# A two-layer decoder trunk on one core: the second MLP product in 16 full steps round a ring, last steps in turn, first six products side by side

## The chip, the cores and the metric

The kernel runs on one core of one Trainium2 chip. The metric is the device time of one execution in microseconds, as the median over several runs. The engines are called PE (matrix products), DVE (vector), ACT (scalar, activations and copies), POOL (general) and SP, whose queue issues most transfers. PSUM banks hold what PE accumulates; SBUF holds everything else.

## The reference

Each of the two layers does, on 1024 tokens of 1024 channels in f32 (positions, pooling and rotary tables left out here):

```python
for i in range(DEPTH):
    hn = rmsnorm(h, norm1[i])
    z = hn @ w_in[i]
    ...
    pool_out = pool_mixer(u, pool_w[i], pool_scale[i])
    attn_out = dilated_mixer(q, k, v)
    h = h + jnp.concatenate([pool_out, attn_out], axis=-1) @ w_out[i]
    hn = rmsnorm(h, norm2[i])
    h = h + jnp.square(jax.nn.relu(hn @ w_up[i])) @ w_down[i]
    gate = jax.nn.sigmoid(rmsnorm(h, norm3[i]) @ w_gate[i])
    h = h + gate * (p[i] @ w_ple[i])
return rmsnorm(h, final_norm)
```

`dilated_mixer` joins three head groups by a softmax over their log-sums; the MLP has 4096 inner channels, so `w_up` is 1024 x 4096 and `w_down` 4096 x 1024. The two products with them are what the change is mostly about.

## The kernel before, in words

**Numbers.** Every f32 operand of a large product is split into a high and a low part (fp32r). ACT makes the high part by a copy, DVE the low part by a subtraction, and PE does three matmuls of 128x128 by 128x512 for each pair of tiles (high-high, high-low, low-high).

**Seven products for eight.** The two MLP products are done in blocks of 2 x 2 tiles with seven products, P1 to P7, in place of eight. Class `Seven` prepares the weights: `load` (L261) fetches a set's raw blocks (names u0r, u1r for the up product of layer 0, d0r for the down product) by SP, `sums` (L274 to L287) makes four sums of blocks on POOL (u0s, d0s), `make` (L289 to L301) makes each of the seven pieces (u0p, d0p): ACT copies (L299), DVE subtracts (L301). `products7` (L527 to L537) issues the matmuls (L535). The other side of the product are the pieces xP (of the normalised residual, four row tiles, for the up product) and wP (of the squared ReLU, for the down product).

**The banks.** P1, P6, P5 and P3 of a set accumulate one after another in a bank X (three buffers), P7 and P4 in a bank Z (two), P2 in a bank Y (two); the order is P1, P7, P6, P2, P5, P4, P3. A product's result must be taken out of its bank (`close`) before the next product of that bank may go on in it. At one product of four row tiles, twelve matmuls, X's next product follows one other product later.

**Up product** (`class Up`, L1129 to L1182): 16 sets of 256 inner channels ("channel pairs"), seven products each over the four row tiles xs. `close` copies on ACT or adds on DVE into y, then ReLU times the norm factor on DVE (L1156), square on ACT (L1159), four differences ys on DVE (L1174 to L1180), and SP writes the seven pieces to x_d in memory.

**Down product** (`class Down`, L1199 to L1219): 19 steps of `STEPS`, triples (t, a, b): output pair t (of 4) takes row tiles a to b of the 16. The first three steps have 3, 2 and 1 row tiles, then come 13 steps of 4, then three with 3, 2 and 1. `close` adds a bank into an SBUF accumulator acc on DVE (L1212). `x_back` (L1189 to L1196) brings one wP piece of one row tile back: SP transfer, ACT copy (L1194), DVE low part (L1196). After each product of a step, one piece of one new row tile is fetched. When an output pair has its last row tile, `rest` splits the result for the gate product and adds its squares to the third norm.

**Around them.** Ahead of the up product lies the output projection (bank names po, evacuated by L1025 and L1048 on DVE into res), which needs the attention outputs. These are weighed with jt, a 96x128 transpose of the joint weights (L907), written to memory and spread by DMA (wb). Behind the down product comes the gate product (gt) with ss_c, the norm's column sums.

**What sets the order.** A class `Clock` runs generators on a simulated time at build, and the kernel's instructions come out in the order of that time; the numbers in the generators (`yield 900.0`) and in the lead times of `Seven` are delays in ns that decide only this order. On the chip every engine runs its own instructions in that order and waits on semaphores for the others.

Of the kernel before, what the change touches and what calls it, by code (L numbers as in the profile page):

```python
# [37 lines left out]
T_M1, W_0, W_1 = 13000.0, 6000.0, 1800.0  # L38
# [3 lines left out]
STEPS = [(3, 0, 3), (2, 0, 2), (1, 0, 1)] + [(a % 4, a, min(a + 4, 16)) for a in range(16)]  # L42
# [72 lines left out]
def body(nc, tc, pools, A, out):  # L115
# [107 lines left out]
    class Seven:  # L223
# [26 lines left out]

        def lead(self, ns, step):

            for q in sorted(k for k in self.kicks if k < 0):
                for fn in self.kicks[q]:
                    ck.at(max(0.0, ns + q * step), fn)

        def at(self, q):
            for fn in self.kicks.get(q, ()):
                fn()

        def load(self, j):  # L261
            src, k0, n, c0 = self.sets[j]
            self.raw[j] = []
            for t in range(2):
                r = blk(f"{self.name}r{t}", F32, (128, n, 2, 128))
                nc.sync.dma_start(out=r.rearrange("p i k c -> p (i k) c"),
                                  in_=src[256 * k0:256 * (k0 + n), c0 + 128 * t:c0 + 128 * t + 128]
                                  .rearrange("(k p) c -> p k c", p=128))
                self.raw[j].append(r)

# [3 lines left out]
        def sums(self, j):  # L274
            a11, a12, a21, a22 = (self.block(j, t, k) for t in range(2) for k in range(2))
            n = self.sets[j][2]
            s = [blk(f"{self.name}s0", F32, (128, 2, n, 128))]
# [1216 lines left out]
```

## Time and profile before

| | |
|---|---|
| median of 3 runs | 2368.24 us (2368.02 to 2368.82) |
| profiled execution | 2371.95 us |
| its span | 2370.2 us, mean granted clock of PE 0.988 |
| PE busy | 2296.6 us (97%) |
| DVE busy | 1704.2 us (72%) |
| ACT, POOL busy | 1008.5 us (43%), 709.3 us (30%) |
| stages of layer 1 | up 422.6 to 741.4 us, down 741.4 to 1067.5 us |
| stages of layer 2 | up 1585.4 to 1906.0 us, down 1906.0 to 2232.2 us |

The profile is one execution. Durations are those of its instructions; a wait is the time in which an engine stood still before an instruction, put down to what released it last. The granted clock of PE is given as a share of full speed: 0.5 is 1.2 GHz, 1.0 is 2.4 GHz. PE matmuls overlap, so a row's own length (0.39 us) is more than the distance between two starts. The rows that the prediction rests on stand below in their own section.

### The profile page before, as it was taken

What the parts mean: (1) busy time and instruction counts of PE and PEld (TensorE: products, weight loads), DVE (VectorE), ACT (ScalarE), POOL (GpSimd) and SP (SyncE); (2) the same over time, 40 slices, a digit from 0 to 9 for tenths busy, and PEclk for the clock granted to TensorE, in tenths of its full rate; (3) what the DMA queues carried; (4) which work ended last, traced back from release to release, by engine and by line L of the source; (5) the groups of instructions that cost most, each with busy time, mean ns of one, the idle gap of its engine ahead of it and who ended that gap; (6) DMA issues with size and microseconds to landing.
All of it is one profiled execution on the core that took longest, in us unless ns stands there. A gap on an engine that the chain in (4) does not pass through costs nothing.

```text
span 2370.2 us, 30970 instructions
## 1 busy us (share of the span) xinstructions
PE 2296.6 (97%) x11088; PEld 1850.2 (78%) x11088; DVE 1704.2 (72%) x2888; ACT 1008.5 (43%) x2161; POOL 709.3 (30%) x562
## 2 busy tenths in 40 slices
PE   8999999899999999989999999999999989999898
PEld 6767778788887788878887767887888868888788
DVE  7555657687778888886565466686777798888845
ACT  5244533443335344444324345334433354443545
POOL 5111126323331433341221122253233233332422
PEclk9999999999999999999999999999999999999999
DMA  5011133254448555521120112233444485553214
GB/s 178 19 46 19 38 90 107 67 165 158 155 150 282 162 159 158 150 67 45 59 58 19 37 37 56 81 116 98 154 156 156 152 289 151 159 156 107 85 54 134
DMA packets 292401, 268.31 MB, mean 113 GB/s; under 512 B 12092, under 2 KB 223672, under 8 KB 292248
## 3 DMA queue, kind: packets, MB, share of 16 engines
q1 hardware_dynamic: 289656, 262.70, 36.3%
q0 software_dynamic: 2272, 3.61, 0.9%
q8 instruction: 87, 1.43, 0.2%
q14 instruction: 66, 0.54, 0.1%
q10 hardware_dynamic: 320, 0.03, 0.0%
HBM read 193.65 MB, written 72.58 MB: 112 GB/s over the span
## 4 chain that ended last, share of the span: by engine, by line
PE 46%; DVE 5%; ACT 1%; POOL 1%; issue 1%; DMA 1%; SPq 0%; DVEq 0%; ACTq 0%; POOLq 0%
PE X L535 13%; PE Z L535 7%; PE Y L535 3%; PE in L520 3%; PE in L518 3%; PE in L522 3%; PE gt L522 2%; PE gt L518 2%; PE gt L520 2%; PE s L752 1%; PE o L788 1%; PE e L774 1%; PE pl L518 1%; PE pl L520 1%; PE pl L522 1%
## 5 line engine op out<-in xcount | busy, mean ns | idle before, releaser
L535 PE MATMUL X<-wP,d1p 128*128 128x512 f32 x768 | 187.6, 394 | 14.5 <-DVE acc L1212 13.9
L535 PE MATMUL X<-wP,d0p 128*128 128x512 f32 x768 | 188.5, 395 | 13.1 <-DVE acc L1212 12.0
L535 PE MATMUL X<-xP,u0p 128*128 128x512 f32 x768 | 185.5, 394 | 3.9 <-ACT y L1133 3.9
L535 PE MATMUL X<-xP,u1p 128*128 128x512 f32 x768 | 185.1, 393 | 3.9 <-ACT y L1133 3.9
L1196 DVE TENSOR_TENSOR wP<-wP 128x512 fp32r<-128x512 f32 x224 | 184.0, 824 | 3.9 <-ACT wP L1194 3.9
L535 PEld LDWEIGHTS X<-wP,d1p 128*128 128x128 f32 x768 | 144.3, 190 | 49.9 <-ACT d1p L299 9.0
L535 PEld LDWEIGHTS X<-wP,d0p 128*128 128x128 f32 x768 | 144.5, 190 | 49.2 <-ACT d0p L299 9.6
L535 PEld LDWEIGHTS X<-xP,u0p 128*128 128x128 f32 x768 | 145.9, 190 | 35.2 <-ACT y L1133 4.7
L535 PEld LDWEIGHTS X<-xP,u1p 128*128 128x128 f32 x768 | 145.4, 190 | 35.1 <-ACT y L1133 4.8
L1159 ACT ACTIVATE y<-y 128x1024 f32<-128x1024 f32 x64 | 67.5, 1055 | 221.9 <-DVE y L1156 221.9
L1194 ACT ACTIVATE wP<-wP 128x512 fp32r<-128x512 f32 x224 | 137.9, 620 | 40.5 <-DMA wP<-x_d 40.2
L188 DVE SCALAR_TENSOR_TENSOR wl<-wr,gt,wh 128x128 fp32r<-128x128 f32 (+1 forms) x288 | 118.8, 444 | 38.7 <-ACT wh L194 38.4
L647 POOL TENSOR_TENSOR rot<-rot,s 128x512 f32<-128x512 f32 x48 | 61.5, 1285 | 277.3 <-DVE rot L645 216.2
L1212 DVE TENSOR_TENSOR acc<-acc,X 128x512 f32<-128x512 f32 x152 | 103.6, 682 | 34.1 <-PE X L535 30.5
L765 ACT ACTIVATE sm<-sm,nm 128x128 f32<-128x128 f32 (+1 forms) x192 | 84.5, 442 | 93.1 <-DVE nm L762 92.9
L194 ACT ACTIVATE wh<-wr,gt 128x128 fp32r<-128x128 f32 (+1 forms) x304 | 104.2, 396 | 0.7 <-DMA wr<-in_w_in_dram 0.7
L758 DVE CUSTOM_DVE_ANT_0 sm<-s,cst 128x128 f32<-128x128 f32 (+1 forms) x192 | 58.3, 347 | 52.0 <-PE s L752 52.0
L535 PE MATMUL Z<-xP,u1p 128*128 128x512 f32 x384 | 95.0, 396 | 0.3 <-DVE xP L1011 0.2
L535 PE MATMUL Z<-xP,u0p 128*128 128x512 f32 x384 | 93.8, 392 | 0.3 <-DVE xP L1011 0.2
L535 PE MATMUL Z<-wP,d0p 128*128 128x512 f32 x384 | 93.5, 390 | 0.0
L535 PE MATMUL Z<-wP,d1p 128*128 128x512 f32 x384 | 93.4, 389 | 0.0
L535 PEld LDWEIGHTS Z<-xP,u1p 128*128 128x128 f32 x384 | 73.2, 191 | 16.3 <-DVE xP L1011 0.5
(474 smaller groups left out, 5969.0 us busy)
## 6 DMA issues: line engine op xcount, KB each, us to landing
wP<-x_d SPq DMA_DIRECT2D x224, 256.0 KB, 2.8
x_d<-ys SPq DMA_DIRECT2D x64, 512.0 KB, 3.5
wr<-in_w_in_dram SPq DMA_DIRECT2D x40, 512.0 KB, 3.8
u0r<-in_w_up_dram SPq DMA_DIRECT2D x32, 512.0 KB, 5.4
x_d<-y SPq DMA_DIRECT2D x32, 512.0 KB, 2.8
u1r<-in_w_up_dram SPq DMA_DIRECT2D x32, 512.0 KB, 5.6
d0r<-in_w_down_dram SPq DMA_DIRECT2D x26, 512.0 KB, 5.7
d1r<-in_w_down_dram SPq DMA_DIRECT2D x26, 512.0 KB, 5.7
```

What stands on the lines that cost most here:

```text
L188: nc.vector.scalar_tensor_tensor(l[:, k], raw[:, k], gs[k], f(h[:, k]), op0=OP.mult, op1=OP.subtract)
L194: nc.scalar.activation(h[:, k], raw[:, k], AF.Copy, scale=gs[k])
L518: nc.tensor.matmul(p, wh, h[:, cols], start=first and i == 0, stop=False)
L520: nc.tensor.matmul(p, wh, l[:, cols], start=False, stop=False)
L522: nc.tensor.matmul(p, wl, h[:, cols], start=False, stop=last and i == n - 1)
L535: nc.tensor.matmul(p, w[:, a, i], x[:, b], start=first and i == 0 and a == b == 0, stop=i == n - 1 and a == 1, skip_group_check=not first)
L647: nc.gpsimd.tensor_tensor(a, a, tb["s"][:, hs(hf)], op=OP.mult)
L765: nc.scalar.activation(sm[:, i, hh], sm[:, i, hh], AF.Exp, bias=nm[:, j:j + 1], scale=0.125, accum_out=ml[g][:, n, 4 + h:5 + h])
L1159: nc.scalar.activation(y, y, AF.Square)
L1194: nc.scalar.activation(t[:, 0], f(t[:, 1]), AF.Copy)
L1196: nc.vector.tensor_tensor(t[:, 1], f(t[:, 1]), f(t[:, 0]), op=OP.subtract)
L1212: nc.vector.tensor_tensor(a, a, p, op=OP.add)
```

## The change

1. **STEPS.** 16 steps of four row tiles each, in a ring: steps 2n and 2n+1 take the row tiles 2n to 2n+3 (wrapping behind 16) for two of the four output pairs, alternately pairs 0, 1 and 2, 3. Weights that wrap are loaded by two transfers. Pieces of two new row tiles are fetched in odd steps (`t % 2`), the second 5000 ns behind the first in the build's time; the first four row tiles are fetched during the last 14 up products.
2. **In turn.** The last two down steps, and the last two channel pairs of the up product, are issued product by product in turn (P1 of the one, P1 of the other, P7, P7, ...). What follows each finished result (`rest`) is collected in `ends` and handed out three at a time per product of the last step. The differences ys of the last two channel pairs come 24000 ns later in the build's time.
3. **Side by side.** The first six up products (P1, P2, P7 of two channel pairs) are interleaved on each row tile (before: four), and the last four output-projection results take banks of the kinds mm, o, e, e in place of s, s, e, e (s holds Y, e holds Z, mm holds X).
4. **Times.** `Seven` starts its parts by build time and no longer by product number; several delays change (the joint weights, the spreading, the norms, x_back).

```diff
+ORDER = ("P1", "P7", "P6", "P2", "P5", "P4", "P3")
+
+STEPS = [(2 * (i // 2 % 2) + i % 2, i // 2 * 2, 4) for i in range(16)]
...
+        def __init__(self, sets, seq, name, lead=(12, 6, 4), side=0):
             self.sets, self.seq, self.name = sets, seq, name
             load, sums, make = lead
             self.raw, self.sum, self.piece = {}, {}, {}
             self.first = {}
+            self.begin, t = [], 0.0
             for q, (j, _) in enumerate(seq):
                 self.first.setdefault(j, q)
-            self.kicks = {}
+                self.begin.append(t)
+                t += 675.0 * sets[j][2]
+            self.kicks = []
             for j, q in self.first.items():
-                self.kick(q - load, lambda j=j: self.load(j))
-                self.kick(q - sums, lambda j=j: ck.go(self.sums(j)))
+                self.kick(q, load, lambda j=j: self.load(j))
+                self.kick(q, sums, lambda j=j: ck.go(self.sums(j)))
             for q, (j, P) in enumerate(seq):
-                self.kick(q - make, lambda j=j, P=P: ck.go(self.make(j, P), (name, j, P)))
-
-        def kick(self, q, fn):
-            self.kicks.setdefault(q, []).append(fn)
-
-        def lead(self, ns, step):
-
-            for q in sorted(k for k in self.kicks if k < 0):
-                for fn in self.kicks[q]:
-                    ck.at(max(0.0, ns + q * step), fn)
-
-        def at(self, q):
-            for fn in self.kicks.get(q, ()):
-                fn()
+                fn = lambda j=j, P=P: ck.go(self.make(j, P), (name, j, P))
+                if q < side:
+                    self.kicks.append((-9000.0 + 1200.0 * q, fn))
+                else:
+                    self.kick(q, make, fn)
+            self.kicks.sort(key=lambda x: x[0])
...
+            yield 7000.0
...
-        first = [(0, "P1"), (1, "P1"), (0, "P2"), (1, "P2"), (0, "P7"), (0, "P6"), (1, "P7"), (0, "P5"),
-                 (1, "P6"), (0, "P4"), (1, "P5"), (0, "P3"), (1, "P4"), (1, "P3")]
+        first = [(j, P) for P in ("P1", "P2", "P7", "P6", "P5", "P4", "P3") for j in range(2)]
         n7 = len(sevens[L][0])
-        seq = first + [(j, P) for j in range(2, n7) for P in ("P1", "P7", "P6", "P2", "P5", "P4", "P3")]
-        S7 = Seven(sevens[L][0], seq, f"u{L}")
+        seq = first + [(j, P) for j in range(2, n7 - 2) for P in ORDER]
+        seq += [(j, P) for P in ORDER for j in (n7 - 2, n7 - 1)]
+        S7 = Seven(sevens[L][0], seq, f"u{L}", side=6)
...
-        outs = [(bank(f"po{L}", ("s", "e")[k // 2]), wk(ws[k % 2], range(8)), hs(k // 2)) for k in range(4)]
+        outs = [(bank(f"po{L}", ("mm", "o", "e", "e")[k]), wk(ws[k % 2], range(8)), hs(k // 2)) for k in range(4)]
...
+                if self.j >= n7 - 2:
+                    yield 24000.0
...
+            nc.sync.dma_start(out=f(t[:, 1]), in_=x_d[i % 16][PLACE[P]])
+            yield 6000.0
...
+                    if self.j >= nst - 4 and P in ("P2", "P3", "P4", "P5"):
+                        ends.append((self, a, m, hf))
...
+        def end(n):
+
+            for i in range(min(n, len(ends))):
+                s, a, m, hf = ends.pop(0)
+                if m not in hg3:
+                    hg3[m] = pair(f"g3_{m}_{L}")
+                ck.go(s.rest(a, m, hf), (id(hg3[m][0]), hf), 800.0 + 1300.0 * i)
+
+        nst = len(STEPS)
+        seq2 = [(k, P) for k in range(nst - 2) for P in ORDER]
+        seq2 += [(k, P) for P in ORDER for k in (nst - 2, nst - 1)]
         D7 = Seven(sevens[L][1], seq2, f"d{L}", (9, 6, 3))
...
-        run(S7, seq, range(4), live, lambda j: xs)
-        for q in range(4, len(seq)):
+        run(S7, seq, range(6), live, lambda j: xs)
+        for q in range(6, len(seq)):
             run(S7, seq, [q], live, lambda j: xs)
             if q == len(seq) - 8:
-                D7.lead(7 * 12 * 225.0, 2700.0)
-                early = [(i, P) for P in ORDER for i in range(3)] + [(3, P) for P in ORDER]
-                for n, (i, P) in enumerate(early):
-                    ck.at(3200.0 + 1150.0 * n, lambda i=i, P=P: ck.go(x_back(i, P)))
-
-
-        live = {k: Down(k) for k in range(len(STEPS))}
-        for q in range(len(seq2)):
-            k, P = seq2[q]
-            s = live[k]
+                D7.lead(8 * 12 * 225.0)
+            n = q - len(seq) + 15
+            if n > 0 and n % 2 == 0:
+                for i in range(4):
+                    ck.at(1500.0 * i + 300.0 * n, lambda i=i, P=seq[q][1]: ck.go(x_back(i, P)))
+
+
+        live = {k: Down(k) for k in range(nst)}
+        for q, (k, P) in enumerate(seq2):
+            t, a, n = STEPS[k]
             if P == "P1":
-                for m in (2 * s.t, 2 * s.t + 1):
+                for m in (2 * t, 2 * t + 1):
                     if acc[m] is None:
                         acc[m] = blk(f"acc{m}_{L}")
                         nc.sync.dma_start(out=acc[m], in_=h_d[m])
-                if s.b == 16:
-                    if norm3 is None:
-                        norm3 = Norm(f"c{L}")
-                    for m in (2 * s.t, 2 * s.t + 1):
-                        hg3.append(pair(f"g3_{m}_{L}"))
-            run(D7, seq2, [q], live, lambda k: xw[STEPS[k][1]:STEPS[k][2]])
-            if k >= 3 and s.a + 4 < 16:
-                ck.go(x_back(s.a + 4, P))
+                if k >= nst - 2 and norm3 is None:
+                    norm3 = Norm(f"c{L}")
+            run(D7, seq2, [q], live, lambda k: xw[a:a + n])
+            if t % 2 and k < nst - 2:
+                ck.go(x_back(a + 4, P))
+                ck.at(5000.0, lambda i=a + 5, P=P: ck.go(x_back(i, P)))
+            if k == nst - 1:
+                end(3 if P != "P3" else 16)
```

Three places show what moves. Line numbers are those of each kernel: L301 of before is L332 of the changed one, L1048 is L1079, L1050 is L1081, L1015 is L1046, L1196 is L1230, L1212 is L1242, L535 is L566. X, Y and Z are the banks, acc_0_... the accumulators of layer 0, po_3696 and po_3697 the results of the last output projection for the first half of the tokens, po_3698 and po_3699 for the second.

DVE, end of layer 0's output projection and start of its up product, before:

```order
L301 TENSOR_TENSOR u0p<-u0r_3701,u0p 128x512
L301 TENSOR_TENSOR u0p<-u0r_3705,u0p 128x512
L1048 TENSOR_TENSOR res_0_3856<-po_3696,h_6H 128x512
L1048 TENSOR_TENSOR res_0_3857<-po_3697,h_7H 128x512
L1050 TENSOR_TENSOR res_0_3856<-res_0_3856,h_6L 128x512
L1050 TENSOR_TENSOR res_0_3857<-res_0_3857,h_7L 128x512
L1015 SCALAR_TENSOR_TENSOR xP_3861<-res_0_3856,gt,xP_3861 128x512
L1015 SCALAR_TENSOR_TENSOR xP_3864<-res_0_3857,gt,xP_3864 128x512
L301 TENSOR_TENSOR u0p<-u0s_3756,u0p 128x512
L301 TENSOR_TENSOR u0p<-u0s_3779,u0p 128x512
L301 TENSOR_TENSOR u0p<-u0s_3775,u0p 128x512
L301 TENSOR_TENSOR u0p<-u0s_3756,u0p 128x512
```

The same place in the changed kernel:

```order
L332 TENSOR_TENSOR u0p<-u0r_3705,u0p 128x512
L332 TENSOR_TENSOR u0p<-u0s_3756,u0p 128x512
L332 TENSOR_TENSOR u0p<-u0s_3775,u0p 128x512
L1079 TENSOR_TENSOR res_0_3862<-po_3696,h_6H 128x512
L1079 TENSOR_TENSOR res_0_3863<-po_3697,h_7H 128x512
L1081 TENSOR_TENSOR res_0_3862<-res_0_3862,h_6L 128x512
L1081 TENSOR_TENSOR res_0_3863<-res_0_3863,h_7L 128x512
L1046 SCALAR_TENSOR_TENSOR xP_3867<-res_0_3862,gt,xP_3867 128x512
L1046 SCALAR_TENSOR_TENSOR xP_3870<-res_0_3863,gt,xP_3870 128x512
L1079 TENSOR_TENSOR res_0_3862<-po_3698,h_6H 128x512
L1079 TENSOR_TENSOR res_0_3863<-po_3699,h_7H 128x512
```

Two low parts of sums moved ahead of the first results, and the second half's results follow the first half's xP at once, where four low parts stood before. PE meanwhile, in the changed kernel, on the first row tile:

```order
L566 MATMUL X_3888<-xP_3271,u0p 128x512 x3
L566 MATMUL X_3889<-xP_3271,u0p 128x512 x3
L566 MATMUL Y_3890<-xP_3339,u0p 128x512 x3
L566 MATMUL Y_3891<-xP_3339,u0p 128x512 x3
L566 MATMUL Z_3892<-xP_3392,u0p 128x512 x3
L566 MATMUL Z_3893<-xP_3392,u0p 128x512 x3
```

Z comes as the 13th matmul; its two banks are those of po_3698 and po_3699. They were so before too, but there Z began behind all 48 matmuls of X and Y.

DVE inside the down product of layer 0, before, in a step of four row tiles:

```order
L1212 TENSOR_TENSOR acc_0_6512<-acc_0_6512,Y_7412 128x512
L1196 TENSOR_TENSOR wP_7385<-wP_7385 128x512
L301 TENSOR_TENSOR d0p<-d0r_7298,d0p 128x512
L1212 TENSOR_TENSOR acc_0_6514<-acc_0_6514,X_7344 128x512
L1196 TENSOR_TENSOR wP_7408<-wP_7408 128x512
L301 TENSOR_TENSOR d0p<-d0s_7363,d0p 128x512
```

The changed kernel, from the last products of an even step into an odd one:

```order
L1242 TENSOR_TENSOR acc_0_6762<-acc_0_6762,X_6766 128x512
L332 TENSOR_TENSOR d0p<-d0s_6669,d0p 128x512
L1230 TENSOR_TENSOR wP_6781<-wP_6781 128x512
L1242 TENSOR_TENSOR acc_0_6760<-acc_0_6760,Y_6830 128x512
L332 TENSOR_TENSOR d0p<-d0r_6724,d0p 128x512
L1230 TENSOR_TENSOR wP_6803<-wP_6803 128x512
L1242 TENSOR_TENSOR acc_0_6762<-acc_0_6762,X_6766 128x512
L332 TENSOR_TENSOR d0p<-d0s_6783,d0p 128x512
L1230 TENSOR_TENSOR wP_6822<-wP_6822 128x512
L1230 TENSOR_TENSOR wP_6826<-wP_6826 128x512
L1242 TENSOR_TENSOR acc_0_6762<-acc_0_6762,Z_6787 128x512
L332 TENSOR_TENSOR d0p<-d0s_6809,d0p 128x512
```

Where each product had one close, one wP and one low part of a weight piece, the products of the other half of a pair of steps now have no wP, and these have two.

PE at the end of layer 0's down product, before, the last step:

```order
L535 MATMUL X_8800<-wP_8279,d0p 128x512 x3
L535 MATMUL Z_8810<-wP_8303,d0p 128x512 x3
L535 MATMUL X_8800<-wP_8326,d0p 128x512 x3
L535 MATMUL Y_8830<-wP_8347,d0p 128x512 x3
L535 MATMUL X_8800<-wP_8367,d0p 128x512 x3
L535 MATMUL Z_8810<-wP_8391,d0p 128x512 x3
L535 MATMUL X_8800<-wP_8411,d0p 128x512 x3
```

And in the changed kernel the last two products of the two steps that take turns:

```order
L566 MATMUL Z_8549<-wP_8439,d0p 128x512 x3
L566 MATMUL Z_8549<-wP_8484,d0p 128x512 x3
L566 MATMUL X_8467<-wP_8147,d0p 128x512 x3
L566 MATMUL X_8467<-wP_8194,d0p 128x512 x3
L566 MATMUL X_8467<-wP_8463,d0p 128x512 x3
L566 MATMUL X_8467<-wP_8513,d0p 128x512 x3
L566 MATMUL X_8496<-wP_8147,d0p 128x512 x3
L566 MATMUL X_8496<-wP_8194,d0p 128x512 x3
L566 MATMUL X_8496<-wP_8463,d0p 128x512 x3
L566 MATMUL X_8496<-wP_8513,d0p 128x512 x3
```

A product had three matmuls at the end and X came back after three others; now it has twelve, and the two X banks alternate.

## Rows read from the trace of the kernel before

**Rows 1.** The page: busy us (share) of the engines, and the chain by engine.

```profile
PE 2296.6 (97%) x11088; PEld 1850.2 (78%) x11088; DVE 1704.2 (72%) x2888; ACT 1008.5 (43%) x2161; POOL 709.3 (30%) x562
...
PE 46%; DVE 5%; ACT 1%; POOL 1%; issue 1%; DMA 1%; SPq 0%; DVEq 0%; ACTq 0%; POOLq 0%
```

**Rows 2.** Waits of PE, whole span: us in total, times, longest us.

```profile
PE X L535 <- DVE acc L1212: 25.9, 18, 5.2
PE X L535 <- ACT y L1133: 7.8, 4, 3.1
...
PE o L788 <- ACT v L983: 5.0, 3, 2.4
PE ss_b L437 <- POOL sq_b L426: 3.5, 2, 1.8
PE jt L907 <- DVE cat_1L L506: 2.9, 1, 2.9
PE jt L907 <- DVE cat_0L L506: 2.9, 1, 2.9
PE ss_c L437 <- POOL sq_c L426: 2.3, 4, 0.6
...
PE Y L535 <- DVE res L1048: 1.3, 2, 0.7
...
PE X L535 <- DVE wP L1196: 1.1, 3, 0.5
```

**Rows 3.** Waits of PE in 741:782, 1905:1947 and 1040:1080 us, first row each.

```profile
PE X L535 <- DVE acc L1212: 6.0, 6, 2.0
...
PE X L535 <- DVE acc L1212: 7.5, 6, 2.0
...
PE X L535 <- DVE acc L1212: 6.0, 2, 5.2
```

**Rows 4.** Windows: us; busy us (instructions) of the engines; PEclk; DMA share; GB/s.

```profile
304.60:308.00 3.40, 3.40 (x18) 3.40 (x17) 1.34 (x3) 0.45 (x2) 3.32 (x3) 0.51 0.06 14
...
441.00:446.00 5.00, 4.74 (x14) 3.82 (x15) 2.93 (x5) 4.44 (x10) 3.12 (x2) 0.66 0.00 0
...
748.00:752.00 4.00, 4.00 (x11) 3.18 (x12) 4.00 (x8) 3.38 (x8) 0.00 (x0) 0.57 0.75 283
782.00:1040.00 258.00, 258.00 (x1140) 213.71 (x1139) 218.65 (x285) 108.53 (x190) 85.34 (x58) 1.00 0.47 137
...
1061.00:1066.00 5.00, 4.68 (x11) 3.31 (x12) 4.20 (x10) 1.16 (x3) 1.28 (x1) 0.52 0.47 150
```

**Rows 5.** Timeline of DVE at the up start: start us, us, instruction [idle before].

```profile
423.93 0.68 DVE L1048 TENSOR_TENSOR res<-po,h_6H 128x512 f32<-128x512 f32 x1
...
428.01 2.49 DVE L301 TENSOR_TENSOR u0p<-u0s,u0p 128x512 fp32r<-128x512 f32 x4
```

**Rows 6.** Timeline of DVE within a step of the down product.

```profile
853.85 0.68 DVE L301 TENSOR_TENSOR d0p<-d0s,d0p 128x512 fp32r<-128x512 f32 x1
...
856.57 1.78 DVE L301 TENSOR_TENSOR d0p<-d0s,d0p 128x512 fp32r<-128x512 f32 x1
858.27 0.67 DVE L1212 TENSOR_TENSOR acc<-acc,X 128x512 f32<-128x512 f32 x1
858.87 1.18 DVE L1196 TENSOR_TENSOR wP<-wP 128x512 fp32r<-128x512 f32 x1
...
861.40 1.34 DVE L1196 TENSOR_TENSOR wP<-wP 128x512 fp32r<-128x512 f32 x1
862.66 1.78 DVE L301 TENSOR_TENSOR d0p<-d0s,d0p 128x512 fp32r<-128x512 f32 x1
```

**Rows 7.** Groups, 782:1040 us: shapes, count; busy us, mean ns; idle before.

```profile
L1196 DVE TENSOR_TENSOR wP<-wP 128x512 fp32r<-128x512 f32 x84 | 71.4, 850 | 0.0
L301 DVE TENSOR_TENSOR d0p<-d0s,d0p 128x512 fp32r<-128x512 f32 x52 | 61.8, 1188 | 0.0
...
L285 POOL TENSOR_TENSOR d0s<-d0s,d0r 128x512 f32<-128x512 f32 x12 | 15.6, 1297 | 17.9 <-issue 15.4 <-DVE d0p L301 2.5
```

More of the change, by code (lines that the diff above doesn't have):

```diff
@@ L37 @@
 T_ROT = [3300.0, 15800.0, 17000.0, 17500.0, 19500.0, 27400.0, 28200.0, 29000.0, 29800.0, 30600.0]
-T_M1, W_0, W_1 = 13000.0, 6000.0, 1800.0
+T_M1, W_0, W_1 = 13000.0, 9000.0, 1800.0
 T_W0, T_C, T_G, T_N = 7400.0, 20000.0, 32000.0, 27500.0
-STEPS = [(3, 0, 3), (2, 0, 2), (1, 0, 1)] + [(a % 4, a, min(a + 4, 16)) for a in range(16)]
+ORDER = ("P1", "P7", "P6", "P2", "P5", "P4", "P3")
+STEPS = [(2 * (i // 2 % 2) + i % 2, i // 2 * 2, 4) for i in range(16)]
 SWAP = [(i ^ 8) if i < 16 else i for i in range(32)]
@@ L263, in load, with two, part @@
             self.raw[j] = []
+            rs = self.two("r", n, (n, 2, 128))
             for t in range(2):
[L265 to L268, printed above, removed]
-                self.raw[j].append(r)
+                r = rs[t]()
+                m = min(n, src.shape[0] // 256 - k0)
+                for i, j0, j1 in ((0, k0, k0 + m), (m, 0, n - m)):
+                    if j1 > j0:
+                        nc.sync.dma_start(out=r[:, i:i + j1 - j0].rearrange("p i k c -> p (i k) c"),
+                                          in_=src[256 * j0:256 * j1, c0 + 128 * t:c0 + 128 * t + 128]
+                                          .rearrange("(k p) c -> p k c", p=128))
+                self.raw[j].append(r)
+        def two(self, name, n, shape):
+            if n > 2:
+                return [lambda i=i: blk(f"{self.name}{name}{i}", F32, (128, *shape)) for i in range(2)]
+            b = []
+            def part(i):
+                if not b:
+                    b.append(blk(f"{self.name}{name}", F32, (128, 2, *shape)))
+                return b[0][:, i]
+            return [lambda i=i: part(i) for i in range(2)]
         def block(self, j, t, k):
@@ L276, in sums @@
             n = self.sets[j][2]
-            s = [blk(f"{self.name}s0", F32, (128, 2, n, 128))]
+            ss = self.two("s", n, (2, n, 128))
+            s = [ss[0]()]
             add = nc.gpsimd.tensor_tensor
@@ L283, in sums @@
             yield 1500.0
-            s.append(blk(f"{self.name}s1", F32, (128, 2, n, 128)))
+            s.append(ss[1]())
             add(s[1][:, 0], s[0][:, 1], a11, op=OP.subtract)
@@ L324, in body @@
         sevens.append(([(wu, 0, 4, 256 * j) for j in range(FF // 256)],
-                       [(wd, a, b - a, 256 * t) for t, a, b in STEPS]))
+                       [(wd, a, n, 256 * t) for t, a, n in STEPS]))
         dn0.append(len(groups))
@@ L1106, in layer @@
         outs = ws = w = None
-        norm2.start(14000.0, slack=3000.0)
+        norm2.start(17000.0, slack=3000.0)
         norm3 = None
-        hg3 = []
+        hg3 = {}
         PLACE = {"P1": 0, "P2": 1, "P3": 2, "P7": 3, "P5": 4, "P6": 5, "P4": 6}
@@ L1174, in sums @@
                 sub(s[0][:, 0], b22, b12, op=OP.subtract)
+                yield 700.0
                 sub(s[0][:, 1], b12, b11, op=OP.subtract)
-                yield 1000.0
+                yield 1400.0
                 sub(s[1][:, 0], b22, s[0][:, 1], op=OP.subtract)
+                yield 700.0
                 nc.sync.dma_start(out=d[:, 3:5], in_=s[0])
-                yield 1000.0
                 sub(s[1][:, 1], b21, s[1][:, 0], op=OP.subtract)
-                yield 700.0
+                yield 2000.0
                 nc.sync.dma_start(out=d[:, 5:7], in_=s[1])
-        xw = [{} for _ in range(16)]
+        xw = [{} for _ in range(18)]
         for x in xw:
@@ L1263, in layer @@
                 W.begin(W.i, delay=6000.0)
-        norm3.start(3000.0)
+        norm3.start(7000.0)
         pT = ple_in(L)
```

38 lines of the change are left out of this document (20 added, 18 removed).

## The prediction, made before the changed kernel had run

> **What bounds the kernel now.** I read the page's busy shares first, then its chain, then the waits of PE, then the stretches in which PE waits. PE is busy for 97% of the span, and the next engine, DVE, for 72%; the chain names PE for 46% of the span and DVE for 5% [rows 1]. The reader is to see a row of matmuls with a few holes. The change leaves the number of matmuls as it is (1344 a layer for the second product, before and after), so only the holes can be won.
>
> Rows 2 name the holes. Nine of PE's waits belong to what the diff touches, and they sum to 52.7 us. By place, over both layers: **A**, in the attention stage, jt 5.8 and o behind ACT v 5.0, together 10.8. **B**, at the start of the up product, X behind ACT y 7.8, ss_b 3.5, Y behind res 1.3, together 12.6. **C**, the small steps at the start of the down product, X behind acc 6.0 and 7.5 [rows 3], and X behind wP 1.1, together 14.6. **D**, the end of the down product and the start of the gate, the rest of X behind acc, 12.4 (6.0 of it in layer 1 [rows 3]), and ss_c 2.3, together 14.7.
>
> A hole costs more than its wait, since the granted clock drops to its lower level, 1.2 GHz, behind it. Between 748 and 752 us, after a wait of 2.0, the mean clock is 0.57 and PE starts 11 matmuls in 4.00 us [rows 4]. In the undisturbed stretch 1140 matmuls took 258.00 us [rows 4], which is 0.227 each and **2.72 us** for a product of twelve; 11 need 2.5, so **1.5 us** are lost. The same reading gives 1.5 at 441 us (14 matmuls in 4.74 us) and 2.2 at 1061 us (11 in 4.68) [rows 4]. A layer pays such a stretch once in A (304.6 us) and in C, twice in B and twice in D, one of these of 2.2: over both layers A 3.0, B 6.0, C 3.0, D 7.4.
>
> Holes with clock: A 13.8, B 18.6, C 17.6, D 22.1, **72.1 us** in all. The change can give no more than this, for in between there is nothing to win: from 782 to 1040 us PE is busy for 258.00 of 258 us [rows 4].
>
> **The change part by part.** *A.* The jt matmul stands 27 v2p matmuls and 8 o matmuls later. 18 v2p matmuls took 3.40 us at half the clock [rows 4], so 27 take at least 2.6 at the full one, and the o matmuls come on top: about the 2.9 us for which jt waited. ACT's v copies now stand ahead of the cat halves that waited for the weights' DMA. I keep 1.0 us of wait and 0.5 of clock a layer. Saved 13.8 − 3.0 = 10.8.
>
> *B.* The first six products run side by side (X, X, Y, Y, Z, Z on each row tile). X's P1 is then finished 15 matmuls, 3.4 us, ahead of X's next use, so the 3.1 us that P6 waited for its copy goes; ss_b stands 85 matmuls into the stage instead of about 75, with ACT's squares ahead of the copies. The first two results leave Y's banks, which ends the wait of Y. In their place comes **a new wait**: Z's banks still hold the last two out-projection results, and Z now starts at the 13th matmul instead of the 49th, 2.7 us after the up product began at 422.6, at 425.3 us. Ahead of that evacuation DVE has six low parts (four before), two results, two additions and two xP rows. The first result was taken at 423.93, behind a low part, and these six operations lasted until 428.01, 4.1 us [rows 5]. Two more low parts (0.60 each) give 425.1, the six 429.2, the evacuation itself 429.8. If the low parts are done before 422.6 it is 427.3. I take the later one, since the low part ahead of the result was late in the trace too: 4.5 + 1.5 of clock, 6.0 a layer (between 3.5 and 8 if ACT is late as well). Saved 18.6 − 12.0 = 6.6.
>
> *C.* The 3-, 2- and 1-tile steps go; all 16 steps are four tiles wide and a product is always 2.72 us. DVE has to add an X result into acc before the next X product, one product of another bank later: a slack of 2.72 − 0.60 = **2.1 us**, where 0.60 is the distance of two DVE starts [rows 6]. What DVE does there is counted in the order. From the close of P2 of the last channel pair but one to the close of P3 of step 0 it has 54 instructions of 0.60, two of twice the width (1.2 each) and two sets of POOL sums. A set costs DVE what rows 6 show: low parts of 1.78 twice and wP of 1.18 and 1.34 beside it, instead of 0.68, so 3.4 us. That makes 32.6 + 2.4 + 6.8 = 41.8 us against 14 products, 38.1: 3.7 over, less the slack 1.6. The ten deferred subtractions of ys then meet three products (8.2 us) together with six other instructions and a set: 9.7 + 3.4 = 13.1, 4.9 over, less the slack 2.8. Together 4.4 a layer, 8.8 for both (2 to 8 a layer as ends: slack twice as large, or clock and one set more). Saved 8.8.
>
> *The ring.* Each pair of steps now makes its 14 wP pieces in one stretch, from P2 of the odd step to P5 of the even one: 30 DVE instructions (14 wP, 8 closes, 8 low parts) in 8 products, 21.8 us. They need 30 x 0.603 + 3.4 = **21.5**. Before, every product had three (1.8 of 2.72). It fits, with the slack in reserve. A wP piece is fetched seven products (19 us) ahead of its use; its copy and low part are 1.5 us. Over both layers the d pieces fall from 266 to 224 (ACT and DVE), the POOL sets from 38 to 32, wP pieces and their SP transfers rise from 224 to 252; with PE never waiting there before, these cost nothing as long as the stretch holds. I add 1.0 us of stall a layer, 2.0 in all (below at 0; the upper end is a rival).
>
> The Trainium skill, "SBUF — State Buffer", section "Who interferes with whom", has VectorE and GpSimd share a port pair as an exclusive lock: an instruction of VectorE with two SBUF inputs and one of GpSimd that reads SBUF shut each other out, the second for the whole of the first. The trace agrees: the low part that began at 856.57 took 1.78 us, the close from PSUM that followed it beside the next sum 0.67 [rows 6].
>
> *D.* The last two steps take turns product by product, so each bank is used again two products, 5.4 us, later, and no product is 0.68 us short (three matmuls). The jam that held X back for 5.2 us [rows 2] has no place. Normalisation and gate rows are handed out three per product of the last step. ss_c stands 37 matmuls into the gate instead of 22, 3.4 us later, against single waits of 0.6 [rows 2]. I keep one stretch of low clock a layer. Saved 22.1 − 3.0 = 19.1.
>
> **The sum.** 10.8 + 6.6 + 8.8 + 19.1 − 2.0 = **43.3 us**. The profiled run took 2371.95 us (its span 2370.2 and 1.75 around it), 3.7 more than the median of 2368.24. It would become 2328.7, the median **2325**. About 0.2%, 4.7 us, is what a measurement of this kernel can tell from no change.
>
> **The rivals.** *POOL's sums shut DVE out in full.* DVE has no pauses in the heavy stretches, so each of the four sums may meet an instruction: 4 x 1.30 (the shortest sum, L285 [rows 7]) = 5.2 us a set instead of 3.4. The ring's stretch is then 23.3, 1.5 over, inside the slack; C with three sets grows by 5.4 a layer, 11 us: 2336. For it: DVE without pauses. Against it: a sum that finds DVE working waits itself, and POOL has time. Chance 0.15.
>
> *The holes only move.* Z's bank and DVE's queue give back all of B and C: 10.8 + 19.1 − 2.0 = 28 us, 2340. For it: at both places I already count a wait, and a low part or two more in the queue suffices. Chance 0.12.
>
> *Nearly all goes.* The low parts of the up start are early, and the excess in C is taken up by pieces that DVE may run later; of 72.1 some 8 stay: 64 us, 2304. For it: 28% of DVE is idle. Chance 0.12.
>
> *The ring makes DVE the bound: slower.* There are 14 pairs of steps. The gain is gone when a pair stalls for 43.3/14 = 3.1 us, that is when the 30 instructions need 21.8 + 2.1 + 3.1 = 27.0 us, 0.90 each. With the means of the steady stretch (wP 0.850, low parts of sums 1.188 [rows 7], closes 0.68) they need 14 x 0.85 + 8 x 1.19 + 8 x 0.68 = 26.9. At 4.5 us a pair it is 63 − 43 = 20 us slower, 2388. Against it: those means hold the contention of two sets for 14 wP, and one set falls into the stretch. Chance 0.06, and 0.05 that the stall is some 3 us and nothing is left to see.
>
> The forecast itself has 0.50, with 2312 to 2336 as its own range from the ends of B and C. Faster by over 0.2%: 0.50 + 0.15 + 0.12 + 0.12 = 0.89; the same 0.05; slower 0.06. The range takes in the forecast and the three rivals that are faster: **2302 to 2344**.
>
> **What would show it.** Right: jt and P6 without a wait; at 425 us Z behind DVE's res for 2 to 4.5 us; X behind acc for some 4 us at the start of each down product, hardly anything inside the ring, no hole of 5 us at its end; DVE's wP rows in bundles of two in odd steps. Wrong: X behind acc in every second step, or X behind wP anywhere in the ring.

## The result, and the profile after

| | before | changed |
|---|---|---|
| median of the runs | 2368.53 us (4 runs) | 2334.41 us (4 runs, 2332.01 to 2337.91) |
| profiled execution, its span | 2371.95, 2370.2 us | 2332.01, 2330.2 us |

The ratio of the runs is 0.9851, with a 95% interval of 0.9829 to 0.9872: 34 us faster where 43 were forecast (2325; range 2302 to 2344). The profiled executions lie further apart (40.0 us of span) than the medians, since the one of before was 3.4 us above the median of its four runs and the one of the changed kernel was its fastest run.

Page of the changed kernel, busy us of the engines and the chain [compare rows 1]:

```profile
PE 2280.8 (98%) x11088; PEld 1841.8 (79%) x11088; DVE 1677.5 (72%) x2832; ACT 1014.7 (44%) x2147; POOL 694.3 (30%) x538
...
PE 82%; DVE 8%; DMA 3%; POOL 2%; ACT 2%; issue 2%; SPq 0%; DVEq 0%; ACTq 0%; POOLq 0%
```

Waits of PE, whole span: us in total, times, longest us [compare rows 2]:

```profile
PE X L566 <- DVE acc L1242: 19.2, 14, 5.1
PE Z L566 <- DVE res L1079: 9.1, 2, 4.6
...
PE X L566 <- ACT y L1164: 0.8, 2, 0.4
...
PE X L566 <- DVE d0p L332: 0.4, 1, 0.4
```

jt, o behind ACT v, ss_b and ss_c, which stood in rows 2 with 17 us, are gone from the list; X behind ACT y fell from 7.8 to 0.8 us. Z behind res is new. X behind acc fell only from 25.9 to 19.2. The attention stage, from the first v2p matmul to the first po matmul, took 38.4 and 38.0 us and now takes 31.0 in both layers; the up product 319.1 and 320.6, now 315.3 and 315.2; the down product 325.8 and 325.9, now 320.6 and 320.7 (from the first matmul of a stage to the first of the next). That is 14.4, 9.2 and 10.4 us less over both layers; the gate and what follows each down product give 5.7, the rest 0.3, together the 40.0 of the two spans.

Where in the down product the 10.4 us came from is told by three windows of layer 1, before and then changed: its first 252 matmuls (21 products of twelve, where C lies), the next 924 (the ring) and the last 168 (where D lies). Columns: us; busy us of PE, PEld, DVE, ACT, POOL, with instructions (PE counts one or two more at a window's edge); PEclk; DMA share; GB/s.

```profile
741.64:810.28 68.64, 61.95 (x254) 47.54 (x252) 63.88 (x97) 33.22 (x64) 24.37 (x20) 0.98 0.73 240
810.28:1019.72 209.44, 209.44 (x926) 173.48 (x924) 179.92 (x232) 87.22 (x151) 68.16 (x44) 1.00 0.51 148
1019.72:1067.47 47.75, 41.38 (x169) 32.50 (x168) 39.99 (x60) 23.42 (x48) 20.88 (x18) 0.93 0.25 76
```

```profile
730.12:799.76 69.64, 61.23 (x253) 49.17 (x252) 53.82 (x83) 30.77 (x53) 19.59 (x14) 0.95 0.79 260
799.76:1011.94 212.18, 210.98 (x926) 173.03 (x924) 167.54 (x230) 88.96 (x155) 68.72 (x47) 1.00 0.51 156
1011.94:1050.75 38.81, 38.41 (x169) 31.45 (x168) 37.41 (x47) 26.27 (x46) 15.27 (x11) 1.00 0.24 76
```

In layer 2 the same stretches went from 69.1 to 69.3, from 209.4 to 212.6 and from 47.3 to 38.8 us. So the end of the down product gained 17.4 us over both layers, its start lost 1.2 and the ring lost 5.9.

Where X still waits in layer 1, by windows of 730:760, 760:800 and 800:1020 us, first row each [compare rows 3]:

```profile
PE X L566 <- DVE acc L1242: 5.1, 1, 5.1
...
PE X L566 <- DVE acc L1242: 3.2, 1, 3.2
...
PE X L566 <- DVE acc L1242: 1.2, 5, 0.2
```

The ring has five short waits a layer, one in the heavy stretch of each of five pairs of steps, 1.2 us in layer 1 and 1.6 in layer 2 (1.0 was allowed). They cost more than their length. The second of them on PE:

```profile
860.16 2.88 PE L566 MATMUL Z<-wP,d0p 128*128 128x512 f32 x12
863.28 1.42 PE L566 MATMUL X<-wP,d0p 128*128 128x512 f32 x5 [0.24 <-DVE acc L1242]
```

Twelve matmuls at the steady distance of 0.227 are over in 2.72, so X could have started at 862.88 and not at 863.28: 0.40 lost for a recorded wait of 0.24, which is counted only from the end of the last row. Five of these make most of the 2.7 and 3.2 us by which the ring is longer than the same 924 matmuls were before. The end of the down product has only the wait of 0.4 behind d0p. Nearly all the rest of the waits is at the start of the down product, one in step 0 and one in step 2. DVE shows what they are. Its timeline there (start us, us, instruction, idle before and what ended it):

```profile
736.67 0.69 DVE L1230 TENSOR_TENSOR wP<-wP 128x512 fp32r<-128x512 f32 x1
740.40 0.69 DVE L1242 TENSOR_TENSOR acc<-acc,X 128x512 f32<-128x512 f32 x1 [3.05 <-DMA acc<-h_d]
...
783.66 0.69 DVE L1242 TENSOR_TENSOR acc<-acc,X 128x512 f32<-128x512 f32 x1 [4.42 <-DMA acc<-h_d]
```

The chain of waits through the first of them (start us, us, what):

```profile
734.29 6.01 DMA acc<-h_d
...
740.40 0.70 DVE acc L1242
741.10 0.14 issue
741.24 4.38 PE X L566 x12
```

DVE stood idle for 3.05 and 4.42 us, its queue done, until the accumulator's first value (the residual, h_d) had landed. In the program the transfer is issued where its step begins (730.12 us on PE). SP, whose queue follows (start us, us, transfers), came to it only at 734.29, behind two blocks of weights and two wP pieces, and beside these it took 6.0 us. A product of twelve matmuls lasts 2.7.

```profile
728.85 0.42 SPq L1226 DMA_DIRECT2D wP<-x_d  x1
729.32 1.78 SPq L284 DMA_DIRECT2D d0r<-in_w_down_dram  x2
731.32 1.01 SPq L1199 DMA_DIRECT2D x_d<-y  x1
732.44 1.75 SPq L1226 DMA_DIRECT2D wP<-x_d  x2
734.29 1.23 SPq L1290 DMA_DIRECT2D acc<-h_d  x2
```

### The profile page after: what moved, and what is told of

It is laid out like the page before. It is cut to its first block, busy times and chain, and to the rows that moved or that the text cites. A ratio compares the mean times of both kernels' runs of the same rounds, so it can differ in the third digit from the quotient of the medians.

```text
span 2330.2 us, 30901 instructions
## 1 busy us (share of the span) xinstructions
PE 2280.8 (98%) x11088; PEld 1841.8 (79%) x11088; DVE 1677.5 (72%) x2832; ACT 1014.7 (44%) x2147; POOL 694.3 (30%) x538
## 4 chain that ended last, share of the span: by engine, by line
PE 82%; DVE 8%; DMA 3%; POOL 2%; ACT 2%; issue 2%; SPq 0%; DVEq 0%; ACTq 0%; POOLq 0%
PE X L566 27%; PE Z L566 12%; PE Y L566 7%; PE in L551 6%; PE in L549 6%; PE in L553 5%; PE gt L553 2%; PE gt L551 2%; PE gt L549 2%; PE s L783 2%; PE o L819 2%; DVE wP L1230 2%; DMA wP<-x_d 2%; PE e L805 1%; POOL res L1058 1%
## 5 line engine op out<-in xcount | busy, mean ns | idle before, releaser
L1230 DVE TENSOR_TENSOR wP<-wP 128x512 fp32r<-128x512 f32 x252 | 197.5, 808 | 0.9 <-ACT wP L1228 0.9
L566 PE MATMUL X<-wP,d1p 128*128 128x512 f32 x768 | 186.2, 395 | 10.2 <-DVE acc L1242 9.7
L566 PE MATMUL X<-wP,d0p 128*128 128x512 f32 x768 | 186.2, 395 | 10.0 <-DVE acc L1242 9.5
L566 PE MATMUL X<-xP,u0p 128*128 128x512 f32 x768 | 183.2, 391 | 0.4 <-ACT y L1164 0.4
L566 PE MATMUL X<-xP,u1p 128*128 128x512 f32 x768 | 183.1, 391 | 0.4 <-ACT y L1164 0.4
L566 PEld LDWEIGHTS X<-wP,d0p 128*128 128x128 f32 x768 | 145.5, 191 | 44.4 <-DVE acc L1242 6.9
L566 PEld LDWEIGHTS X<-wP,d1p 128*128 128x128 f32 x768 | 145.4, 190 | 44.6 <-DVE acc L1242 7.2
L566 PEld LDWEIGHTS X<-xP,u0p 128*128 128x128 f32 x768 | 144.6, 189 | 30.9 <-ACT y L1164 0.8
L566 PEld LDWEIGHTS X<-xP,u1p 128*128 128x128 f32 x768 | 144.6, 189 | 30.9 <-ACT y L1164 0.8
L1228 ACT ACTIVATE wP<-wP 128x512 fp32r<-128x512 f32 x252 | 147.3, 617 | 24.6 <-DMA wP<-x_d 22.2
L1242 DVE TENSOR_TENSOR acc<-acc,X 128x512 f32<-128x512 f32 x128 | 87.4, 683 | 77.9 <-PE X L566 63.8
L566 PE MATMUL Z<-xP,u0p 128*128 128x512 f32 x384 | 93.5, 393 | 4.6 <-DVE res L1079 4.6
L566 PE MATMUL Z<-xP,u1p 128*128 128x512 f32 x384 | 93.5, 393 | 4.5 <-DVE res L1079 4.5
L566 PE MATMUL Z<-wP,d0p 128*128 128x512 f32 x384 | 91.9, 389 | 0.0
L566 PE MATMUL Z<-wP,d1p 128*128 128x512 f32 x384 | 91.9, 389 | 0.0
L330 ACT ACTIVATE d0p<-d0s 128x512 fp32r<-128x512 f32 x64 | 40.1, 628 | 111.9 <-PE X L566 65.7
```

The source lines that it names most:

```text
L566: nc.tensor.matmul(p, w[:, a, i], x[:, b], start=first and i == 0 and a == b == 0, stop=i == n - 1 and a == 1, skip_group_check=not first)
L1228: nc.scalar.activation(t[:, 0], f(t[:, 1]), AF.Copy)
L1230: nc.vector.tensor_tensor(t[:, 1], f(t[:, 1]), f(t[:, 0]), op=OP.subtract)
L1242: nc.vector.tensor_tensor(a, a, p, op=OP.add)
```

## The experiments

All are edits of the changed kernel; times are medians. Each is beside runs of before on the same chip (2369.9 to 2371.4 us), so the ratios can be compared.

**r0, the changed kernel again.**

> The changed kernel again, beside the others on this chip: about 2334 us, with holes at the start of the up product (Z behind res 4.6 us a layer) and at the start of the down product (X behind acc 5.1 and 3.2 us a layer).

2334.97 us, ratio 0.9852 (0.9837 to 0.9866). The waits are the same, 19.5 us for X and 9.2 for Z, but its profiled span is 2335.0 us against 2330.2. What differs is the clock behind the same holes. The 6.8 us behind the wait of step 2, in the first profile and here (us; busy us of PE, PEld, DVE, ACT, POOL, with instructions; PEclk; DMA share; GB/s):

```profile
784.40:791.20 6.80, 6.79 (x23) 5.42 (x24) 6.05 (x10) 2.71 (x5) 0.00 (x0) 0.75 0.85 245
```

```profile
786.70:793.50 6.80, 6.80 (x18) 5.40 (x19) 5.43 (x10) 2.71 (x5) 0.00 (x1) 0.58 0.72 190
```

The same stretch holds 23 matmuls in the first profile and 18 here (30 at full speed): the mean clock was 0.75 and 0.58, so the low level, 0.5, lasted for about half of it in the one and for most of it in the other.

**e1, acc fetched early.** (`load_acc`, new, issues the two transfers of a step.)

```diff
...
+            if q in (len(seq) - 7, len(seq) - 6):
+                load_acc(q - len(seq) + 7)
...
-                for m in (2 * t, 2 * t + 1):
-                    if acc[m] is None:
-                        acc[m] = blk(f"acc{m}_{L}")
-                        nc.sync.dma_start(out=acc[m], in_=h_d[m])
+                if k in (1, 2):
+                    load_acc(k + 1)
```

> The accumulators' first values are fetched earlier: those of steps 0 and 1 behind the 7th and 6th last up product, those of steps 2 and 3 one step ahead. Theory 1, the transfer of acc makes the holes at the start of the down product: both waits go (8.3 us a layer) with two stretches of low clock (3.0), so 22 us less than the changed kernel, about 2312. Theory 2, DVE's queue makes them, as the prediction had it: 4.4 us a layer stay, so 2321 or more. Theory 3, the memory traffic of that time is the limit whatever the order: the wait moves to wP or d0p and the time stays near 2334.

2321.36 us, ratio 0.9794 (0.9780 to 0.9809): 13.6 less than r0, a gain, but not 22. X behind acc falls to 12.9 us. What is left, on PE and DVE in step 0:

```profile
738.49 4.53 PE L566 MATMUL X<-wP,d0p 128*128 128x512 f32 x12 [3.01 <-DVE acc L1247]
...
786.02 3.02 PE L566 MATMUL X<-wP,d0p 128*128 128x512 f32 x12 [1.63 <-DVE acc L1247]
```

```profile
735.98 1.76 DVE L1230 TENSOR_TENSOR wP<-wP 128x512 fp32r<-128x512 f32 x1
737.67 0.67 DVE L1247 TENSOR_TENSOR acc<-acc,X 128x512 f32<-128x512 f32 x1
```

DVE no longer idles before acc; it comes to it late. The waits of 3.0, 1.6 and 0.2 us sum to 4.8 in layer 1, and to 5.6 in layer 2, beside the 4.4 a layer of the prediction for DVE's excess. So both theories hold, one on top of the other: the transfer ended the wait, and behind it stood the queue.

**e12, acc early and ys at once** (the `yield 24000.0` ahead of the differences ys made 700.0, on e1).

> The early fetch of acc together with the differences ys at once. Theory 1, with acc there in time DVE's amount of work is the limit at the start of the down product: eight subtractions, 4.8 us, more ahead of the first results, so the waits of X behind acc grow from 3.0 + 1.6 to some 6 + 0 us a layer, and the time from 2321 to about 2325. Theory 2, the transfers are the limit: the ys transfers no longer stand beside the weights and acc of step 2, as in the run with ys at once alone (4.5 us less), and the time falls to about 2317.

2329.28 us, ratio 0.9831 (0.9818 to 0.9845), 7.9 more than e1 where theory 1 had 4. Theory 1 holds for the place: the waits are now 6.4 us in step 0 and 0.2 in step 2.

```profile
743.23 5.43 PE L566 MATMUL X<-wP,d0p 128*128 128x512 f32 x12 [6.35 <-DVE acc L1247]
```

Eight subtractions more stand ahead of the first result, and PE waits for them there: 3.0 + 1.6 us became 6.4 + 0.2. So putting ys off, as the change does, is worth 7.9 us once acc is there in time.

**e6, ys at once with acc late.**

> The changed kernel with the differences ys of the last two channel pairs made at once instead of 24000 ns later. Theory, the excess of DVE's work at the start of the down product counts: eight subtractions more, 4.8 us, stand ahead of the first acc, but the transfer of acc ends the wait there in any case (DVE stood 3.1 us without work before it), so 2 us or so more a layer, about 2338. If DVE is not near its limit there: no change, and the later holes get shorter.

2330.10 us, ratio 0.9828 (0.9812 to 0.9845), 5 less than r0 where 3 more were expected. The two intervals just overlap; all four runs lie below all eight of the changed kernel. In 720:800 us X waits as long as in r0 (e6 first, then r0):

```profile
PE X L566 <- DVE acc L1242: 8.6, 3, 5.3
...
PE X L566 <- DVE acc L1242: 8.7, 2, 5.6
```

The wait is now in three parts of 5.3, 2.3 and 0.9, and DVE does not wait for acc at all: it comes to each acc after the transfer has landed. The work of the queue fills the time of the transfer. In layer 2 it is the same (7.6 us of X, 8.2 in r0, none of DVE's behind acc). The waits being nearly equal, most of the 5 us must lie in the clock behind them: in the 6.8 us behind the wait of step 2 it is 1.00 here, 0.58 in r0, for a wait of 0.9 instead of 3.1 us.

```profile
786.50:793.30 6.80, 6.80 (x30) 5.65 (x31) 6.80 (x12) 1.27 (x2) 0.00 (x0) 1.00 0.55 168
```

That this holds for every run of e6 is not shown; the profile of the changed kernel, with a clock of 0.75 there, is only 0.8 us longer than that of e6.

**e8, acc early, later wP.** (On e1; `d` is the delay between the fetch and the split.)

```diff
...
-                    ck.at(1500.0 * i + 300.0 * n, lambda i=i, P=seq[q][1]: ck.go(x_back(i, P)))
+                    ck.at(1500.0 * i + 300.0 * n, lambda i=i, P=seq[q][1], d=6000.0 if n < 8 else 10000.0: ck.go(x_back(i, P, d)))
```

> The early fetch of acc, and the wP pieces that are fetched during the last seven up products are split 4000 ns later in the build's time, which puts three of DVE's wP rows behind the first acc of the down product. Theory, what is left of the hole with the early fetch (3.0 us in layer 1) is DVE's queue: three rows of 0.6 less, 1.2 us left, and with fewer or shorter stretches of low clock 4 to 6 us less than with the early fetch alone, about 2316. Rival, it is not DVE's amount of work but the memory traffic (acc or wP landing late): no change from 2321.

2326.25 us, ratio 0.9812 (0.9798 to 0.9827): no gain against e1 (the intervals overlap, and its median is the higher one). The wait at P6 of step 0 did fall, from 3.0 to 0.3 us, but a wait of 3.0 came back two products later:

```profile
735.43 3.00 PE L566 MATMUL X<-wP,d0p 128*128 128x512 f32 x12 [0.32 <-DVE acc L1247]
...
744.13 1.17 PE L566 MATMUL X<-wP,d0p 128*128 128x512 f32 x4 [2.98 <-DVE acc L1247]
```

The pieces put back met POOL's sums there. The expectation was right on the row and wrong on the time: here the excess stayed when three of its rows came later. In e1, too, the four sums lie there (735.7 to 742.3 us) and draw DVE's rows out; what a later set of sums would give, no run shows.

**e2, Z two row tiles later; e7, banks emptied at once; e10, the norm later too.** In `products7` the outputs of P7 lag by two row tiles when several products run side by side; e7 also calls `close` when a product's last matmul is issued; e10 adds the third edit.

```diff
-        for i in range(n):
-            for p, w, P, first in outs:
+        turn = [(i + (2 if P == "P7" and len(outs) > 1 else 0), j, i) for i in range(n)
+                for j, (_, _, P, _) in enumerate(outs)]
+        for _, j, i in sorted(turn):
+            for p, w, P, first in outs[j:j + 1]:
...
+                if i == n - 1:
+                    done(j)
...
-        norm2.start(17000.0, slack=3000.0)
+        norm2.start(22000.0, slack=3000.0)
```

> Of the first six products Z's two come two row tiles behind X's and Y's, so that Z starts at the 37th matmul, 8.2 us into the up product, when the bank has been free for 0.8 us. Theory 1, only Z's bank makes the hole: 4.6 us of wait and some 2 of clock go in each layer, 13 us less than the changed kernel, about 2321. Rival, DVE is behind there whatever PE does first: the wait comes back at X's fourth row tile or at Z's, and no more than 4 us are gained.

> Z two row tiles late as in the second run, and each of the first six products is taken out of its bank as soon as its own last matmul is issued, so that ACT's copies of X stand ahead of the squares and of two xP copies. Theory, the hole of 4.6 us had only moved to ACT's queue: both waits go, some 12 us less than the changed kernel, about 2322. Rival, the last xP pieces are late as well (the combination of the last two residual tiles on DVE is the real limit): the wait moves to X or Z behind xP, and no more than 5 us are gained.

> Z two row tiles late, results taken out at once, and the norm's column sums ss_b start 5000 ns later in the build's time. Theory, every step of this stage has one more that is late: with ss_b some 26 matmuls (6 us) later its waits of 3.0 and 2.0 us go too and nothing else is behind it, 12 us less than the changed kernel, about 2323. Rival, the wait moves on again (to the ReLU that needs the norm, and so to X or Y): 2330 or more.

2331.65 (0.9837, 0.9823 to 0.9852), 2336.20 (0.9855, 0.9840 to 0.9869) and 2330.57 us (0.9834, 0.9816 to 0.9851): none is clear of r0. The first row is the changed kernel, then e2 and e7, each PE's wait at the start of the up product:

```profile
422.31 2.90 PE L566 MATMUL Z<-xP,u0p 128*128 128x512 f32 x6 [4.56 <-DVE res L1079]
```

```profile
435.46 4.63 PE L568 MATMUL X<-xP,u0p 128*128 128x512 f32 x10 [4.17 <-ACT y L1166]
```

```profile
437.86 1.05 PE L468 MATMUL ss_b<-one,sq_b 128*128 128x1 f32 x8 [3.02 <-POOL sq_b L457]
440.87 1.87 PE L468 MATMUL ss_b<-one,sq_b 128*128 128x1 f32 x8 [1.96 <-POOL sq_b L457]
```

and e10, two rows of its waits in the whole span:

```profile
PE X L568 <- ACT y L1173: 5.1, 2, 2.5
PE X L568 <- DVE y L1180: 1.9, 2, 1.5
```

The wait goes from Z's bank to ACT's copies, to POOL's squares, to the next copies of X, with 4 to 5 us a layer each time until the last, where it is 3.5. The rivals were right on the time three times. On the engine only e10's was: in e2 the rival named DVE and it was ACT, in e7 it named the xP pieces and it was POOL.

**e3 and e11, the two places together** (e1 with e2; e8 with e10).

> Both edits. If the holes are independent the gains add: about 2299 us. If the earlier up product runs into a transfer that is late anyway, some of one gain is lost: 2305 to 2312.

> All edits of the two runs above. If the two places are independent the gains add: some 18 us at the down product and 12 at the up product off the changed kernel, about 2304 us. If one of the two theories falls, the sum of what is left of them.

2324.29 (0.9808, 0.9792 to 0.9825) and 2321.97 us (0.9794, 0.9778 to 0.9810). Neither beats e1; e11 is level with it. The sums that were expected did not come, since neither the moves at the up product nor the later wP gave anything clear of the noise by themselves.

**e4, the attention stage's old delays.**

> The changed kernel with the four old delays of the attention stage (jt, its write, the spreading, W_0), so that jt and the v copies stand where they stood before. Theory, these delays alone removed the waits of A: jt 2.9 and o some 2.5 us come back in each layer with a stretch of low clock, so 13 to 15 us more than the changed kernel, about 2349. Rival, A came out of the banks or of the other times: no more than 3 us more.

2349.97 us, ratio 0.9914 (0.9899 to 0.9929): 15.0 more than r0. The waits are those of before [rows 2]:

```profile
PE o L819 <- ACT v L1014: 4.9, 4, 2.1
PE jt L938 <- DVE cat_0L L537: 2.9, 1, 2.9
PE jt L938 <- DVE cat_1L L537: 2.8, 1, 2.8
```

**e5, the last two steps one after the other.**

```diff
-        seq2 += [(k, P) for P in ORDER for k in (nst - 2, nst - 1)]
+        seq2 += [(k, P) for k in (nst - 2, nst - 1) for P in ORDER]
```

> The changed kernel with the last two down steps one after the other instead of in turn. Theory 1, the full width of the steps removed the hole at the end: a product is 2.72 us anyway, X waits for acc 0 to 1 us a layer more and ss_c or the gate a little, 0 to 4 us in all. Theory 2, the turns removed it: a hole of 3 us or more a layer comes back with low clock, 8 us or more, 2343 or above.

2355.72 us, ratio 0.9935 (0.9920 to 0.9950): 20.8 more than r0. Theory 2: the hole of 5 us is back, with steps of full width, and another of 2.3 us before it. PE, and DVE ahead of that acc:

```profile
1044.86 2.98 PE L566 MATMUL X<-wP,d0p 128*128 128x512 f32 x12 [2.32 <-DVE acc L1242]
...
1055.66 5.46 PE L566 MATMUL X<-wP,d0p 128*128 128x512 f32 x12 [5.09 <-DVE acc L1242]
```

```profile
1047.43 3.47 DVE L537 SCALAR_TENSOR_TENSOR g_0L<-acc,gt,g_0H 128x512 fp32r<-128x512 f32 x2
1050.83 0.67 DVE L1242 TENSOR_TENSOR acc<-acc,Y 128x512 f32<-128x512 f32 x1
1051.43 3.48 DVE L537 SCALAR_TENSOR_TENSOR g_0L<-acc,gt,g_0H 128x512 fp32r<-128x512 f32 x3
1054.84 0.68 DVE L1242 TENSOR_TENSOR acc<-acc,X 128x512 f32<-128x512 f32 x1
```

Handed out three per product of a single step, the gate rows jam DVE while POOL adds the norm's squares beside them without a pause (eight of them in 13.6 us from 1038.42): two g rows take 3.47 us instead of two times 0.74. In turn, there are two products for every three. The turns also bring a bank back two products later; which of the two effects counts for more, no run tells, and a thinner handing out without turns was not tried. The additions from PSUM stay at 0.67 in the midst of it. By the Trainium skill, "SBUF — State Buffer", section "Who interferes with whom", an instruction of VectorE with two SBUF inputs and one of GpSimd that reads SBUF wait for each other in full; the trace agrees, with 1.7 us for a g row beside a sum and 0.74 alone.

## Why the prediction was right, and where not

The sign and the range held, and so did the mechanism in A, B and D; C had the wrong wait. The gain was 34 us by the medians instead of 43, and 40.0 between the two profiles from which the sum was worked. That 40.0 is so near 43.3 is partly luck: A, B and D (with what follows it) gave about 10 us more than the sum, C and the ring 14 less. e4 takes A back and e5 the turns of D; no run takes back B's edit or the ring alone, so these two rest on the lengths of their stages. Point by point:

- **A** was forecast to save 10.8 us; no wait of jt or of o behind v is left, and the stage is 7.4 and 7.0 us shorter, 14.4 together, a little more than the 13.8 at which the whole hole was priced. e4 shows that the delays did it (15.0). The 1.5 us a layer kept as a precaution were not needed.
- **B**: the new wait of Z was forecast at 4.5 us a layer and is 4.56. The order of DVE's queue and the durations of rows 5 gave it: in the changed kernel the evacuation of Z's bank began at 421.47, 6.6 us after the up product began (6.6 by the sum). The stage as a whole became 9.2 us shorter where 6.6 were forecast. That the hole is one of several of like size, each behind the next, was not seen; e2, e7 and e10 showed it.
- **C** is the step that failed. It was to save 8.8 us; the first 252 matmuls of the down product became 1.2 us longer over both layers. The waits there are 16.4 us over both layers (14.6 before). The low clock behind them comes on top: the sum had 1.5 us a layer for it before and none for what stays, and the mean clock of the stretch fell from 0.98 to 0.95. The step said "X behind acc" would be what DVE has to do, 41.8 us against 38.1. That term was near in size (e1: 4.8 and 5.6 us in its place; 4.4 forecast), though by luck in part: of its two pieces, 1.6 in step 0 came out as 3.0 and 4.2 in the two layers, and 2.8 with the ys as 1.8 and 1.4 (ten subtractions were counted there; DVE has eight). It was not what ended the wait: the acc transfers were left out of the sum. They are issued with their step. The trace of before had the price: between 741 and 760 us an acc transfer took 6.5 us from issue to landing. In step 0 they stand in the queue behind weights of full width, in step 2 behind the ys that the change had put off to that time (in e6, where these come earlier, DVE waits for no acc).
- **The ring**: forecast 1.0 us a layer; the waits are 1.2 and 1.6, and the stretch is 2.7 and 3.2 longer. DVE did not become the bound. But X behind acc came once in each of five pairs of steps, 38.6 us apart, and "X behind acc in every second step" was named as a sign of being wrong: the stretch does not quite fit, by 0.4 us each time. The low parts of sums, 1.188 us on average before [rows 7], fell to 0.944 within the ring, so the rival of POOL's sums shutting DVE out in full did not come about. In the heavy stretch from 855 to 864 us a set drew DVE's rows out by 3.3 us (3.4 forecast, 5.2 by the rival).
- **D** was forecast to save 19.1 us; the last 168 matmuls of the down product became 17.4 shorter over both layers, and what follows the down product 5.7, not all of it D's. The hole is gone, with a wait of 0.4 us a layer left where 1.5 were kept. Only the reason was half wrong: the prediction gave two, the width and the turns. e5 shows that without the turns the hole comes back at full width.

The sum had no row for how long the low clock lasts. It was put at 1.5 us a hole, and 2.2 for one at the end; behind the same wait the first profile lost 7 matmuls of 30, 1.6 us, and r0 12, 2.7 us. This is a reason for the spread of the runs of the changed kernel, 2332 to 2338 us, and why a prediction to a microsecond is not to be had here.

The fastest version is e1, 2321 us (e11, with more edits, 2322), 13.6 us below the changed kernel and 2.1% below before.

## What to carry to other kernels

When a step moves, list its transfers with their queue and the issue times of what stands ahead, not only its instructions: here fetching ahead a load of 6 us that was issued with its own step gained 13.6 us. When a wait is removed, ask what would end it next and price that too; a hole with three late engines behind it (B) gave nothing clear of the noise for an edit at one or two of them. Work in excess of a stretch stayed when it was put in another order there (e8); moving part of it out of the stretch (e1 against e12, 7.9 us) or taking turns with another step (e5, 20.8 us) helped. A forecast that comes out near is to be checked place by place: here a loss and a surplus nearly cancelled.

## What was not expected of the hardware

Behind the same wait of PE the mean clock of the next 6.8 us was 0.75 in one execution and 0.58 in another (23 against 18 matmuls), so one hole may cost 1.6 us or 2.7. At a DMA share of 1.04 (740 to 745 us) a transfer of acc took 6.0 us from issue to landing. wP pieces, 2.8 as a median over the whole kernel of before, took 5.8 between 728 and 745 us; before, too, they took 4.8 at the start of the down product, so the median of a whole kernel was no guide to this place.
